# Where the convolution taps of a hybrid encoder block stand in VectorE's queue

## The chip, the cores and the metric

The kernel runs on one core of a Trainium2 chip. A core has five engines that run their own queues in order and wait for each other by semaphores: TensorE (PE in the profile, matmuls and transposes; PEld its weight loads), VectorE (DVE), ScalarE (ACT), GpSimd (POOL) and SyncE (SP, which only issues DMAs here). The metric is the device time of one execution in microseconds; lower is better. The number to be predicted is the median of the changed kernel's runs, on the same terms as the median of the kernel before.

## What is computed

One encoder layer on 1024 tokens of width 1024, in float32. Two head groups share one input projection: a convolution group (gated, 31 taps over positions, layer norm, swish) and a neighbourhood attention on a 16 x 64 grid of tokens. Their outputs are concatenated, projected, and a SwiGLU feed-forward follows.

```python
h = rms_norm(x, norm1_g[l])
z = h @ w_in[l]
a, gate, q, k, v = jnp.split(z, splits, axis=-1)
conv_out = conformer_conv(a, gate, dw_kernel[l], dw_bias[l], conv_ln_g[l], conv_ln_b[l])
q = rms_norm(q.reshape(B, S, N_HEADS, HEAD_DIM), q_norm_g[l])
k = rms_norm(k.reshape(B, S, N_HEADS, HEAD_DIM), k_norm_g[l])
attn_out = neighbourhood_attention(q, k, v.reshape(B, S, N_HEADS, HEAD_DIM), rpb[l])
x = x + jnp.concatenate([conv_out, attn_out], axis=-1) @ w_out[l]
h = rms_norm(x, norm2_g[l])
x = x + (jax.nn.silu(h @ w_gate[l]) * (h @ w_up[l])) @ w_down[l]

# in conformer_conv
u = a * jax.nn.sigmoid(gate)
y = conv over positions of u, 31 taps per channel, + dw_bias; layer_norm; silu
```

## The kernel before

Every float32 product is made of three matmuls on a high and a low half of each operand (`mac`, L112 to L114). `split` makes the halves: a ScalarE cast (L104) and a subtraction (L108), on GpSimd for the weights of this stage. Weights are split one chunk at a time by `take()`, in a fixed order.

The stage that matters here is the input projection, up to about 250 us of the span. TensorE makes, one after the other, groups of 24 matmuls (8 blocks of the inner dimension, 3 each):

- key tiles, `project(1, t, head_post)`, t = 0 to 7, 128 tokens each (the first four stand before and among the first gates);
- gate and value halves of the four channel blocks of the convolution, `glu_step(c, h, part, ...)`, c = 0 to 3;
- query tiles, `project(0, t, head_post)`, t = 0 to 7; after each even t a `take()` splits one of the four chunks w20 to w23 of the value weights;
- value tiles, `value(t)`, t = 0 to 7, which read those four chunks in turn, k = 0 to 7, two blocks for each chunk. The first two score matmul pairs (L610) stand ahead of `value(6)` and `value(7)`.

Nothing schedules the instructions but the order in which the Python code issues them. `step(post)` runs the work that belongs to the group before: one group lies between a tile's matmuls and its post-processing. For a key or query tile that is `head_post`: eight ScalarE squares with their sums and a root (`head_sq`, L371, L374), then on VectorE a reciprocal, a scaling and the product zn (`head_scale`, L379, L380, L382). zn is transposed on TensorE (`head_T`, zt, L389) at the end of the group after the next, and ScalarE copies it to qT or kT (L394, L396). For a gate it is a product with the row scales (L442), ScalarE's sigmoid (L443) and a second product (L444); the other half then gives `u` (L450).

The convolution's 31 taps of each of the four channel blocks are done on the side, in two places:

- `conv_taps` does 24 of them on VectorE, in one accumulator `cv` in PSUM: a first product with the bias (L313), 23 multiply-adds (L318), then the sum with the other part (L323). `pump(n)` issues the next n of these, wherever it is called. It stops early where the next block's `u` isn't there yet.
- `side_taps` does the other 7 (SIDE): a product on ScalarE (L343, the first of a block L340) and an add on GpSimd (L344; the first has none). `side()` issues the next one; `step` calls it once at its end.

What is left of the taps is issued by `pump(200)` after `value(5)`, ahead of the first score step (`score_exp`, L623), which takes scores from PSUM, adds the bias table and finds the largest. Score matmuls write into the four PSUM buffers `mm` that the tiles use too, in turn; the second score pair has to wait for a buffer that the first score step frees.

Behind this stage come the attention proper, the output projection and the feed-forward, none of which the change touches. In the changed kernel the same lines stand two or three lines lower (L610 is L613, L623 is L626).

Of the kernel before, what the change touches and what calls it, by code (L numbers as in the profile page):

```python
# [67 lines left out]
def build(ctx, tc, a):  # L68
# [10 lines left out]
    def G(name, dt=F32):  # L79
        return T("G", [P, 1024], 22, name, dt)  # L80
# [7 lines left out]
    def ST(name, dt=F32):  # L88
        return T("st", [P, 512], 5, name, dt)
# [4 lines left out]
    def mm(name):  # L94
        return ps.tile([P, 512], F32, tag="mm", bufs=4, name=name)
# [14 lines left out]
    def mac(acc, l, r, start, stop):  # L110
        (lh, ll), (rh, rl) = l, r
        pe.matmul(acc, lh, rh, start=start, stop=False, skip_group_check=True)  # L112
        pe.matmul(acc, lh, rl, start=False, stop=False, skip_group_check=True)  # L113
        pe.matmul(acc, ll, rh, start=False, stop=stop, skip_group_check=True)  # L114
# [4 lines left out]
    def weave():  # L119
        if woven:  # L120
            woven.pop(0)()
# [228 lines left out]
    def side():  # L350
        next(sides, None)
# [3 lines left out]
    def pump(n):  # L355
        for _ in range(n):
            if not next(conv, False):
                return
# [4 lines left out]
    def head_sq(n, t, z):  # L363
        sq, ss = ST(f"sq{n}{t}"), SM(f"s{n}{t}")
        r = r1[:, t:t + 1]
        if n == 1 and t < 4:
            act.activation(sq, z, AF.Square, scale=r)
            dve.tensor_reduce(ss, sq.rearrange("p (h d) -> p h d", d=HD), mybir.AxisListType.X, OP.add)
        else:
            for h in range(NH):  # L370
                act.activation(sq[:, h * HD:(h + 1) * HD], z[:, h * HD:(h + 1) * HD], AF.Square, scale=r,  # L371
                               accum_out=ss[:, h:h + 1])
        sd = SM(f"d{n}{t}")
        act.activation(sd, ss, AF.Sqrt, bias=eps, scale=1.0 / HD)  # L374
        return sd

    def head_scale(n, t, z, sd):
        r = SM(f"r{n}{t}")
        dve.reciprocal(r, sd)  # L379
        dve.tensor_scalar(r, r, r1[:, t:t + 1], None, op0=OP.mult)  # L380
        zn = ST(f"zn{n}{t}")
        dve.tensor_tensor(zn.rearrange("p (h d) -> p h d", d=HD), z.rearrange("p (h d) -> p h d", d=HD),  # L382
                          r[:, :, None].to_broadcast([P, NH, HD]), OP.mult)
        return zn

    def head_T(n, t, zn):
        pt = tp(f"zt{n}{t}")
        for c in range(4):
            pe.transpose(pt[:, c * P:(c + 1) * P], zn[:, c * P:(c + 1) * P], ident)  # L389
        if n == 0:  # L390
            q5 = qT.rearrange("p c (h b i j) -> p c h b i j", h=2, b=4, j=16)
            p5 = pt.rearrange("p (c i b j) -> p c i b j", c=4, i=2, j=16)
            for i in range(2):
                act.activation(q5[:, :, t // 4, :, 2 * (t % 4) + i, :], p5[:, :, i], AF.Copy, scale=qgs)  # L394
        else:
            act.activation(kT[:, :, t * P:(t + 1) * P], pt.rearrange("p (c s) -> p c s", s=P), AF.Copy, scale=kg)  # L396
# [11 lines left out]
    def step(post=None, n_taps=4):  # L408
        todo = pend[:]
        pend.clear()  # L410
        if post is not None:
            pend.append(post)
        behind()
        for f in todo:
            f(n_taps)
        if not todo:
            pump(n_taps)
        side()

    def head_post(n, t, z):  # L420
        def f(n_taps):
            sd = head_sq(n, t, z)
            pump(2)
            zn = head_scale(n, t, z, sd)
            pump(1)
            woven.extend([lambda: None] * 7)
            woven.append(lambda: head_T(n, t, zn))
        return f

    def glu_step(c, h, part, accs, extra=None):  # L430
        acc = accs[part] = mm(f"gl{c}{h}{part}")
        w = [q.rearrange("p (k m) -> p k m", m=P) for q in wag[1 - part, c][0]]
        for k in range(KB):
            mac(acc, [q[:, k, :] for q in w], [q[:, k, :] for q in hT[h]], k == 0, k == KB - 1)
            weave()
        if extra:
            extra(0)

        def gate(n_taps):
            sg = accs["sg"] = ST(f"sg{c}{h}")  # L440
            row = rb[0][:, h * 512:(h + 1) * 512]
            dve.tensor_tensor(sg, acc, row, OP.mult)  # L442
            act.activation(sg, sg, AF.Sigmoid)  # L443
            dve.tensor_tensor(sg, sg, row, OP.mult)  # L444
            pump(n_taps - 1)

        def val(n_taps):
            if h == 0:
                u.append([G(f"u{c}"), False])
            dve.tensor_tensor(u[c][0][:, h * 512:(h + 1) * 512], acc, accs["sg"], OP.mult)  # L450
            u[c][1] = h == 1
            pump(3)
        step((gate, val)[part])
# [749 lines left out]
    for s, p in enumerate(SEQ):  # L1203
        for k in range(QF - 2):
            n = s * QF + k
# [34 lines left out]
```

## Time and profile before

| | us |
|---|---|
| median of 3 runs | 1081.25 (1081.23 to 1082.03) |
| the profiled execution | 1082.53 |
| its span, first to last instruction | 1080.8 |
| TensorE busy in the span | 1056.1 |
| VectorE busy | 699.0 |
| ScalarE busy | 451.9 |
| GpSimd busy | 392.3 |

The span is what the profile's rows cover. In a row of a timeline stand the start and the duration in us, engine, source line, operation, the tiles written and read, shapes, the number of instructions merged into the row, and in square brackets how long the engine had idled before and what ended that. In a row of the waits stand the total in us, the number of waits and the longest. In a row of the view by windows stand, after the stretch and its length, the busy us and the number of instructions of TensorE, its weight loads, VectorE, ScalarE and GpSimd, then TensorE's granted clock as a share of full speed, the busy share of the DMA engines and their GB/s. TensorE's busy time is modelled from starts, so it overlaps from one matmul to the next: two starts say more than one duration.

### The profile page before, as it was taken

How to read it: one execution, taken by the hardware profiler on the slowest of the kernel's cores; microseconds unless marked ns; L12 is line 12 of the kernel's file. 1: busy time of each engine (PE TensorE's matmuls, PEld its weight loads, DVE VectorE, ACT ScalarE, POOL GpSimd, SP SyncE). 2: the span in 40 equal slices, each digit the busy share in tenths (PEclk: the TensorE clock that was granted, in tenths of full speed). 3: DMA queues.
4: the chain of work that ended last, by engine and by line, in shares of the span. 5: the costliest groups of instructions: out<-in, count | busy, mean ns of one | idle time of the engine just before them, and what ended most of it. 6: DMA issues, size and time to landing. Idle time of an engine off the chain costs nothing.

```text
span 1080.8 us, 14055 instructions
## 1 busy us (share of the span) xinstructions
PE 1056.1 (98%) x5068; PEld 850.7 (79%) x5068; DVE 699.0 (65%) x1055; ACT 451.9 (42%) x988; POOL 392.3 (36%) x303
## 2 busy tenths in 40 slices
PE   7999999989999999999999999999999999999997
PEld 5888888866667888788888888888888888888886
DVE  6768997895765346765646555464564667857883
ACT  6455347725775423533222332223322245433441
POOL 0126665513552301744454544544545300002310
PEclk9999999999999999999999999999999999999999
DMA  8416781234413522022321323322232498624641
GB/s 320 169 48 220 228 243 39 74 143 144 149 59 108 161 102 86 34 88 107 125 100 69 128 97 107 107 98 91 104 126 79 156 333 289 204 88 129 205 133 41
DMA packets 68245, 144.06 MB, mean 133 GB/s; under 512 B 12496, under 2 KB 21200, under 8 KB 67536
## 3 DMA queue, kind: packets, MB, share of 16 engines
q1 hardware_dynamic: 66336, 139.95, 38.3%
q10 hardware_dynamic: 1840, 3.22, 0.9%
q8 instruction: 40, 0.66, 0.2%
q14 instruction: 29, 0.24, 0.1%
HBM read 103.99 MB, written 44.76 MB: 138 GB/s over the span
## 4 chain that ended last, share of the span: by engine, by line
PE 90%; DVE 5%; ACT 3%; issue 1%; DMA 1%; POOL 0%; SPq 0%; ACTq 0%; DVEq 0%
PE B L112 6%; PE B L114 6%; PE B L113 6%; PE D L112 4%; PE D L114 4%; PE D L113 4%; PE A L112 4%; PE A L114 4%; PE A L113 4%; PE z L112 3%; PE z L113 3%; PE z L114 3%; DVE cv L318 3%; PE gl L112 3%; PE gl L114 3%; PE gl L113 3%
## 5 line engine op out<-in xcount | busy, mean ns | idle before, releaser
L318 DVE SCALAR_TENSOR_TENSOR cv<-u,par,cv 128x1009 f32<-128x1009 f32 (+14 forms) x92 | 117.5, 1277 | 2.5
L344 POOL TENSOR_TENSOR pa<-pa,pr 128x1022 f32<-128x1022 f32 (+5 forms) x24 | 57.5, 2395 | 53.8 <-ACT pr L343 53.4
L104 ACT CAST op<-sr 128x512 fp32r<-128x512 f32 x77 | 47.6, 618 | 52.3 <-PE B2d L114 23.2
L1027 DVE TENSOR_TENSOR g<-B,g 128x512 f32<-128x512 f32 x22 | 15.2, 690 | 80.3 <-PE B L114 80.3
L108 DVE TENSOR_TENSOR op<-sr,op 128x512 fp32r<-128x512 f32 x77 | 55.5, 721 | 16.4 <-ACT op L104 16.2
L1195 POOL TENSOR_TENSOR ou<-ou,resm 128x512 f32<-128x512 f32 x8 | 12.9, 1614 | 143.4 <-DMA resm<-xd 142.1
L1036 ACT ACTIVATE D<-D 128x512 f32<-128x512 f32 x22 | 12.8, 582 | 114.5 <-DVE D L1035 114.5
L1022 DVE TENSOR_TENSOR u<-B,g 128x512 f32<-128x512 f32 x22 | 15.2, 691 | 64.5 <-PE B L114 64.5
L104 ACT CAST op<-wd 128x512 fp32r<-128x512 f32 x66 | 40.8, 619 | 30.6 <-DVE wd L1114 18.1
L108 DVE TENSOR_TENSOR op<-wd,op 128x512 fp32r<-128x512 f32 x66 | 52.3, 793 | 2.0 <-ACT op L104 0.2
L876 DVE TENSOR_TENSOR ts<-gu,ts 128x512 f32<-128x512 f32 x44 | 53.1, 1206 | 0.8
L632 POOL TENSOR_SCALAR e<-e,rs 128x288 f32<-128x288 f32 (+1 forms) x64 | 34.1, 545 | 50.4 <-DVE rs L630 37.6
L1025 ACT ACTIVATE A<-A 128x512 f32<-128x512 f32 x20 | 11.6, 582 | 77.4 <-PE A L114 77.4
L625 ACT ACTIVATE e<-e,mx 128x288 f32<-128x288 f32 (+1 forms) x64 | 36.2, 568 | 14.1 <-DVE mx L623 14.1
L641 PEld LDWEIGHTS p<-ident,e 128*96 128x96 f32 (+1 forms) x192 | 20.0, 133 | 18.6 <-issue 10.3
L876 DVE TENSOR_TENSOR ts<-gu 128x512 f32<-128x512 f32 x22 | 33.6, 1528 | 0.0
L623 DVE CUSTOM_DVE_ANT_0 e<-s,tab 128x288 f32<-128x288 f32 (+1 forms) x64 | 29.8, 502 | 5.6 <-PE s L610 5.2
L610 PE MATMUL s<-kT,qT 64*128 64x288 f32 (+1 forms) x128 | 27.6, 496 | 3.8 <-DVE mx L623 3.8
L641 PE MATMUL p<-ident,e 128*96 128x128 f32 (+1 forms) x192 | 27.5, 280 | 3.8 <-DVE pT L646 2.5
L371 ACT ACTIVATE sq<-z,r 128x64 f32<-128x64 f32 x96 | 28.6, 333 | 2.8 <-PE z L114 2.8
L657 PE MATMUL o<-pT,vw 96*64 96x128 f32 (+1 forms) x384 | 28.0, 281 | 0.0
L343 ACT ACTIVATE pr<-u,par 128x1022 f32<-128x1022 f32 (+5 forms) x24 | 27.0, 1137 | 1.6 <-ACT vs L402 1.6
(1034 smaller groups left out, 3469.4 us busy)
## 6 DMA issues: line engine op xcount, KB each, us to landing
gu<-in_gu SPq DMA_DIRECT2D x44, 512.0 KB
sr<-sd SPq DMA_DIRECT2D x77, 256.0 KB
sd<-sd SPq DMA_DIRECT2D x22, 512.0 KB
wd<-in_wd SPq DMA_DIRECT2D x44, 256.0 KB
sd<-g SPq DMA_DIRECT2D x33, 256.0 KB
x<-in_x SPq DMA_DIRECT2D x16, 512.0 KB
xd<-x SPq DMA_DIRECT2D x8, 512.0 KB
resm<-xd SPq DMA_DIRECT2D x16, 256.0 KB
```

Source lines behind the costliest of these rows:

```text
L104: act.copy(hi, src)
L108: eng.tensor_tensor(*[w[..., sl] for w in (lo, src, hi.bitcast(F32))], OP.subtract)
L112: pe.matmul(acc, lh, rh, start=start, stop=False, skip_group_check=True)
L113: pe.matmul(acc, lh, rl, start=False, stop=False, skip_group_check=True)
L114: pe.matmul(acc, ll, rh, start=False, stop=stop, skip_group_check=True)
L318: dve.scalar_tensor_tensor(acc[:, o], uc[:, i], dwk[:, c, t:t + 1], acc[:, o], OP.mult, OP.add)
L344: pool.tensor_tensor(pa[:, o], pa[:, o], pr[:, o], OP.add)
L623: dve.tensor_tensor_reduce(out=e[:, hh], in0=ss[hh], in1=tab[rh, cb][2 * hp + hh], scale=-1.0, scalar=3.0e38, op0=OP.add, op1=OP.min, accu ...
L625: act.activation(e[:, hh], e[:, hh], AF.Exp, bias=mx, scale=-1.0, accum_out=rs[:, hh:hh + 1])
L632: pool.tensor_scalar(es[i][:, hh], es[i][:, hh], rs[:, hh:hh + 1], 1.0, op0=OP.mult, op1=OP.mult)
L641: pe.transpose(pt[:m, g * P:(g + 1) * P], es[i][:, hh, g * m:(g + 1) * m], ident)
L876: dve.tensor_tensor(o, l, r, OP.subtract)
```

## The change

Three places issue the same work in another order. A key or query tile pumps three taps in place of two before `head_scale` (six for key tile 5, five for query tile 1); after it, an odd tile pumps one as before and an even tile none. An odd query tile issues one more side tap. A gate pumps one of its taps between the issue of the sigmoid and the product that needs it. The number of taps and their arithmetic stay as they were.

```diff
     def head_post(n, t, z):
         def f(n_taps):
             sd = head_sq(n, t, z)
-            pump(2)
+            pump(3 + {(1, 5): 3, (0, 1): 2}.get((n, t), 0))
             zn = head_scale(n, t, z, sd)
-            pump(1)
+            pump(t % 2)
+            if n == 0 and t % 2:
+                side()
             woven.extend([lambda: None] * 7)
             woven.append(lambda: head_T(n, t, zn))
         return f
...
             dve.tensor_tensor(sg, acc, row, OP.mult)
             act.activation(sg, sg, AF.Sigmoid)
+            pump(1)
             dve.tensor_tensor(sg, sg, row, OP.mult)
-            pump(n_taps - 1)
+            pump(n_taps - 2)
```

## The prediction

> **What bounds the kernel now.** I read the page first, then the list of waits (TensorE's over the span, VectorE's from 56 to 262 us), then the timeline of each engine around the one wait that the change can reach. A difference of 0.2% (2.16 us) is about what a measurement of this kernel can tell from no change.
>
> ```profile
> PE 1056.1 (98%) x5068; PEld 850.7 (79%) x5068; DVE 699.0 (65%) x1055; ACT 451.9 (42%) x988; POOL 392.3 (36%) x303
> ...
> PE s L610 <- DVE mx L623: 3.8, 1, 3.8
> PE p L641 <- DVE pT L646: 2.5, 5, 0.6
> PE A L112 <- ACT g L1019: 1.9, 1, 1.9
> ...
> DVE r L379 <- ACT d L374: 15.8, 10, 5.3
> DVE sg L444 <- ACT sg L443: 8.4, 8, 2.1
> ```
>
> TensorE (PE) is the bound: it is busy for 1056.1 of 1080.8 us, and its largest wait in mid-kernel is a single one of 3.8 us, for a VectorE (DVE) score step. Only time of TensorE is worth anything here. VectorE's own waits for head squares (15.8 us) and sigmoids (8.4 us) cost nothing by themselves; they matter because VectorE is late at that one place. TensorE's timeline there:
>
> ```profile
> 229.24 0.76 PE L610 MATMUL s<-kT,qT 64*128 64x288 f32 x4
> ...
> 235.71 0.75 PE L610 MATMUL s<-kT,qT 64*128 64x288 f32 x2
> 240.26 0.90 PE L610 MATMUL s<-kT,qT 64*128 64x288 f32 x2 [3.80 <-DVE mx L623]
> ...
> 242.53 0.63 PE L112 MATMUL z<-w20h,hT 128*128 128x512 f32 x1
> 242.96 0.63 PE L113 MATMUL z<-w20l,hT 128*128 128x512 f32 x1
> ...
> 248.26 0.76 PE L610 MATMUL s<-kT,qT 64*128 64x288 f32 x4
> ```
>
> One pair of score matmuls and one value tile take 235.71 - 229.24 = 6.47 us when nothing is in the way. The next pair and tile take 248.26 - 235.71 = 12.55 us. So the wait costs 12.55 - 6.47 = **6.08 us**, not 3.80: another 2.28 us go afterwards, where matmuls start 0.43 us apart (242.53, 242.96). The view by windows shows why; the column behind the five engines is the granted clock:
>
> ```profile
> 236.00:240.00 4.00, 0.46 (x2) 0.01 (x1) 3.86 (x4) 0.00 (x0) 0.00 (x0) 1.00 0.02 8
> 240.80:244.00 3.20, 3.20 (x8) 2.33 (x8) 1.07 (x6) 2.36 (x9) 1.00 (x3) 0.50 0.22 82
> 244.20:248.00 3.80, 3.80 (x18) 3.00 (x16) 0.00 (x0) 0.00 (x0) 0.77 (x2) 1.00 0.00 0
> ```
>
> VectorE is late because it still works off the last convolution channel:
>
> ```profile
> 204.48 0.20 DVE L379 RECIPROCAL r<-d 128x8 f32<-128x8 f32 x1 [0.98 <-ACT d L374]
> ...
> 205.06 0.69 DVE L382 TENSOR_TENSOR zn<-z,r 128x512 f32<-128x512 f32 x1
> 205.66 1.21 DVE L323 TENSOR_TENSOR u<-cv,pa 128x1024 f32<-128x1024 f32 x1
> ...
> 208.30 30.21 DVE L318 SCALAR_TENSOR_TENSOR cv<-u,par,cv 128x1009 f32<-128x1009 f32 x23
> 238.61 1.22 DVE L323 TENSOR_TENSOR u<-cv,pa 128x1024 f32<-128x1024 f32 x1
> 239.75 0.45 DVE L623 CUSTOM_DVE_ANT_0 e<-s,tab 128x288 f32<-128x288 f32 x1
> ```
>
> 23 taps (30.21 us) stand between the last query tile (zn at 205.06) and the first score step (239.75), while inside the tiles before, VectorE idles 0.98 us each time for ScalarE's squares.
>
> **Taps into the waits.** The change adds no VectorE work, it reorders it. By program order 26 instructions follow the last zn before the first score step (a sum, a first product, 23 taps, a sum); afterwards there are 19: 18 taps and a sum. A query tile gets 3 taps (even t) or 4 (odd t) in place of 3, and t = 1 gets 2 more; key tile 5 gets 7 in place of 3. One tap is 30.21 / 23 = 1.313 us, so what follows the last zn takes 18 x 1.313 + 1.14 (238.61 to 239.75) = 24.8 us: begun at 205.66 it ends at 230.4 instead of 239.75. The score row that waits for it can run from 235.71 + 0.35 = 236.1 on. VectorE is then over 5 us early; the 3.80 us are gone, TensorE does not idle there and has no reason to lose its clock: **-6.08 us**. What is late next at that place is TensorE itself.
>
> **One more side tap in odd query tiles.** It puts a second product (L343) on ScalarE and a second add (L344) on GpSimd between the squares of an odd tile and the next weight split (L104, L108). The moved steps issue no DMA. At the last such place, behind the squares of t = 5, the split is that of w23, and TensorE needs its low half soon:
>
> ```profile
> 192.06 0.30 ACT L374 ACTIVATE d<-s,eps 128x8 f32<-128x8 f32 x1
> 192.27 1.13 ACT L340 ACTIVATE pa<-u,par 128x1023 f32<-128x1023 f32 x1
> 193.31 1.03 ACT L104 CAST w23h<-w23r 128x1024 fp32r<-128x1024 f32 x1
> 194.86 0.84 ACT L394 ACTIVATE qT<-zt,qgs 128x256 f32<-128x256 f32 x2 [0.52 <-PE zt L389]
> ...
> 198.31 1.13 ACT L343 ACTIVATE pr<-u,par 128x1022 f32<-128x1022 f32 x1
> ...
> 194.47 2.39 POOL L108 TENSOR_TENSOR w23l<-w23r,w23h 128x1024 fp32r<-128x1024 f32 x1 [4.56 <-issue]
> 199.52 2.40 POOL L344 TENSOR_TENSOR pa<-pa,pr 128x1022 f32<-128x1022 f32 x1 [2.66 <-ACT pr L343]
> ...
> 199.10 0.39 PE L113 MATMUL z<-w23l,hT 128*128 128x512 f32 x1
> ```
>
> Before, this slot holds a channel's first product (L340), which has no GpSimd add, and GpSimd takes w23l at 194.47. In the new program order GpSimd has two adds ahead of w23l. The first can start 199.52 - 198.31 = 1.21 us after its product: 192.27 + 1.21 = 193.48. Two adds of 2.40 end at 198.28, and w23l at 198.28 + 2.39 = 200.67. How long GpSimd's end takes to reach TensorE:
>
> ```profile
> 281.21 0.98 POOL L632 TENSOR_SCALAR e<-e,rs 128x288 f32<-128x288 f32 x2
> ...
> 282.33 0.83 PE L641 MATMUL p<-ident,e 128*96 128x128 f32 x6 [0.36 <-POOL e L632]
> ```
>
> 282.33 - 282.19 = 0.14 us. TensorE can go on at 200.81, where it wanted to at 199.10: **+1.70 us**, a new wait inside the first value tile. TensorE's queue behind it is the rest of that tile, which waits with it, and everything later moves by it, also the last zn (230.4 becomes 232.1, still early). Bounds: 0, if the adds start earlier than I read; not below, since TensorE does not wait there before; and 2.7, if ScalarE's products slip by another 1.0.
>
> **Transposes of the query tiles.** Behind an odd tile's squares ScalarE now has two products and a cast, 0.21 + 1.04 + 1.04 + 1.03 = 3.32 us from 192.06: the next qT starts at 195.38, 0.52 after 194.86, and the squares, the root and r behind it are 0.52 late. In VectorE's queue four taps then stand ahead of an even tile's r: 4 x 1.313 + 1.18 (204.48 to 205.66) = 6.43 us, against the 6.04 of a tile (the two zt rows below); that alone would be 0.39, so ScalarE's 0.52 rules. The room:
>
> ```profile
> 186.35 0.20 DVE L379 RECIPROCAL r<-d 128x8 f32<-128x8 f32 x1 [0.94 <-ACT d L374]
> ...
> 186.93 0.69 DVE L382 TENSOR_TENSOR zn<-z,r 128x512 f32<-128x512 f32 x1
> ...
> 182.15 0.60 PE L389 MATMUL zt<-ident,zn 128*128 128x128 f32 x4
> 188.19 0.60 PE L389 MATMUL zt<-ident,zn 128*128 128x128 f32 x4
> ```
>
> zn ends at 187.62 and, with the same 0.14, is at TensorE by 187.76; the transpose runs at 188.19. Room 0.43, so t = 2 and t = 4 cost 0.52 - 0.43 = 0.09 each (t = 6 lies behind the new wait): **+0.2 us**, between 0 and 0.6. The taps in the key tiles and between a gate's product and its sigmoid's return I take at nothing: they fill VectorE's own waits, and by the list TensorE waits for no key tile and no gate. Were that cover gone, a key tile with four taps ahead would pay the same few tenths, which the 0.6 holds.
>
> **Sum.** -6.08 + 1.70 + 0.2 = -4.18. The profiled execution took 1082.53 us (a span of 1080.8 and 1.73 around it), 1.28 above the median of the runs. On the median of 1081.25 the forecast is **1077.1 us**; in an execution like the profiled one it is a span of 1076.6.
>
> **Does the new wait cost clock as well?** The row to go by is TensorE's other wait:
>
> ```profile
> 435.20 0.74 PE L112 MATMUL A<-h,t0m 128*128 128x512 f32 x1 [1.95 <-ACT g L1019]
> ...
> 438.72 0.40 PE L114 MATMUL A<-h,t0m 128*128 128x512 f32 x1
> 436.00:438.50 2.50, 2.50 (x7) 1.92 (x7) 2.46 (x3) 0.15 (x1) 2.50 (x3) 0.50 0.00 0
> ```
>
> After only 1.95 us of idling the clock was 0.50 until 438.72; 3.52 us at half clock lose 1.76. The waits of up to 0.6 us in the attention show nothing of it. 1.70 lies nearer to 1.95 but is shorter, so the loss is a rival. The Trainium skill (TensorE: Matmul & The Clock Gate, "What's actually happening") halves the clock only after an idle window of about 3.4 us. By that rule the new wait costs no clock and the forecast stands as it is; the wait of 3.80 us agrees, the one of 1.95 us contradicts the rule, and the measurement decides.
>
> **The rivals.**
> - The new wait halves the clock: 1.76 as at 435, up to the 2.28 at 240: 1078.9. For it the row at 435.20, against it the shorter wait. 0.16.
> - Better: GpSimd is not late with w23l, 1077.1 - 1.70 = 1075.4; or the wait at 435, which comes at another moment, keeps its clock, 1077.1 - 1.76 = 1075.3. Nothing in the rows above speaks for the first; the second can't be excluded. Together 0.14.
> - The change doesn't do what it says: the first score step gets no earlier, as something else holds it, its bias table above all, whose buffers are handed on in another order. Then 6.08 stay and 1.9 come on top: 1083.2. Against it: no row shows VectorE waiting for a table before. 0.04.
> - Slower: VectorE becomes the bound of the query tiles. Two tiles hold 7 taps and 2 x 1.18, 11.55 of 12.08 us. From a tap of 1.39 us on, TensorE waits at the transposes; at 1.65 it waits 1.8 per two tiles, 7.3 in all, and the time is 1084.4. Against it: 1.313 is what a tap took, and the change puts no more beside it than one product and one add in two tiles. 0.04.
>
> **How the numbers follow.** The forecast has 0.62. Faster by over 0.2% means below 1079.1: the forecast, the better cases and the clock rival but for its dear end, 0.88. Within 0.2%, up to 1083.4: that end and the table, 0.08. Slower: 0.04. The range leaves out the last two rivals; it goes from 1074.9 (a better case without the 0.2, and 0.2 for the scatter of runs) to 1079.3 (the clock rival with the 0.6 of the transposes).
>
> **What would show it.** Right: no TensorE wait at the score matmuls near 236 and clock 1.00 behind them; a TensorE wait of about 1.7 us for w23l near 199; 18 taps in a row of 23.6 us that end near 231. Wrong: the score wait again, over 0.6 us of TensorE waits at zt, or clock 0.50 behind 200.

## The result, and the profile after

The change made the kernel slower: 1084.78 us in the median of 22 runs (1082.64 to 1086.59) against 1082.75 of the kernel before (22 runs beside them, 1081.23 to 1084.49), a ratio of 1.0021 with a 95% interval of 1.0014 to 1.0028. The forecast was 1077.1 us, 4.2 less than the median of the three runs that it started from; measured are 2.0 more than the kernel before timed beside it. The profiled execution of the kernel after took 1086.28 us, 1.5 above its median, with a span of 1084.6.

The list of waits of the kernel after, TensorE over the span and VectorE from 56 to 262 us as before (engine, tile and line, what it waited for; us in total, times, longest):

```profile
PE zt L389 <- DVE zn L382: 6.0, 3, 2.4
...
PE z L113 <- POOL w23l L108: 1.5, 1, 1.5
...
DVE r L379 <- ACT d L374: 7.1, 6, 3.4
```

The score wait of 3.8 us is off TensorE's list, and VectorE's waits for squares fell from 15.8 to 7.1 us: the taps did move into them. VectorE's timeline ahead of the first score step:

```profile
215.53 23.65 DVE L318 SCALAR_TENSOR_TENSOR cv<-u,par,cv 128x1014 f32<-128x1014 f32 x18
239.28 1.22 DVE L323 TENSOR_TENSOR u<-cv,pa 128x1024 f32<-128x1024 f32 x1
240.43 0.45 DVE L626 CUSTOM_DVE_ANT_0 e<-s,tab 128x288 f32<-128x288 f32 x1
```

18 taps instead of 23. What is new is 6.0 us of waiting for zn, at three transposes. Timelines of VectorE, of GpSimd and of TensorE in the kernel after, around the first two:

```profile
68.64 0.20 DVE L379 RECIPROCAL r<-d 128x8 f32<-128x8 f32 x1
68.88 1.62 DVE L380 TENSOR_SCALAR r<-r,r 128x8 f32<-128x8 f32 x1
...
71.21 7.85 DVE L318 SCALAR_TENSOR_TENSOR cv<-u,par,cv 128x1014 f32<-128x1014 f32 x6
78.97 0.20 DVE L379 RECIPROCAL r<-d 128x8 f32<-128x8 f32 x1
79.20 2.17 DVE L380 TENSOR_SCALAR r<-r,r 128x8 f32<-128x8 f32 x1
81.48 0.69 DVE L382 TENSOR_TENSOR zn<-z,r 128x512 f32<-128x512 f32 x1
...
87.47 2.41 DVE L380 TENSOR_SCALAR r<-r,r 128x8 f32<-128x8 f32 x1
...
68.08 2.39 POOL L344 TENSOR_TENSOR pa<-pa,pr 128x1022 f32<-128x1022 f32 x1 [1.73 <-ACT pr L343]
78.99 2.36 POOL L344 TENSOR_TENSOR pa<-pa,pr 128x1021 f32<-128x1021 f32 x1 [8.52 <-DMA t<-in_rpb]
87.49 2.36 POOL L344 TENSOR_TENSOR pa<-pa,pr 128x1020 f32<-128x1020 f32 x1 [3.82 <-ACT pr L343]
...
82.23 0.66 PE L389 MATMUL zt<-ident,zn 128*128 128x128 f32 x4 [2.25 <-DVE zn L382]
90.82 0.63 PE L389 MATMUL zt<-ident,zn 128*128 128x128 f32 x4 [2.43 <-DVE zn L382]
...
92.33 0.63 PE L112 MATMUL gl<-hT,ag01h 128*128 128x512 f32 x1
92.75 0.63 PE L113 MATMUL gl<-hT,ag01h 128*128 128x512 f32 x1
```

L380 multiplies 128x8 numbers, r by r1. The prediction never named it: it lies between r and zn and takes 0.23 us. Here it takes 1.62, 2.17 and 2.41 us. Its end is each time 0.02 to 0.03 us behind that of the GpSimd add L344 beside it (68.88 + 1.62 = 70.50 and 68.08 + 2.39 = 70.47). The first delay costs TensorE nothing by itself, but it pushes six taps and the next r (78.97) into the next add (78.99). The reciprocal L379 runs at 68.64 in the middle of the same add and still takes 0.20 us. TensorE waits 2.25 and 2.43 us, and behind the second wait its matmuls start 0.42 to 0.43 us apart. The view by windows shows the granted clock there (column behind the five engines), 1.00 behind the first wait and 0.59 behind the second:

```profile
82.30:85.70 3.40, 3.40 (x17) 2.87 (x18) 3.33 (x3) 2.78 (x16) 1.38 (x1) 1.00 1.02 399
91.00:94.20 3.20, 3.20 (x12) 2.59 (x11) 3.13 (x3) 2.71 (x16) 0.00 (x0) 0.59 0.51 147
```

The third wait, and the one for w23l, in the query and the value tiles (GpSimd, VectorE, TensorE):

```profile
180.76 2.39 POOL L108 TENSOR_TENSOR w21l<-w21r,w21h 128x1024 fp32r<-128x1024 f32 x1
206.44 2.37 POOL L108 TENSOR_TENSOR w23l<-w23r,w23h 128x1024 fp32r<-128x1024 f32 x1
...
181.47 1.70 DVE L380 TENSOR_SCALAR r<-r,r 128x8 f32<-128x8 f32 x1
...
184.11 0.63 PE L389 MATMUL zt<-ident,zn 128*128 128x128 f32 x4 [1.30 <-DVE zn L382]
208.87 0.50 PE L113 MATMUL z<-w23l,hT 128*128 128x512 f32 x1 [1.55 <-POOL w23l L108]
```

The additional side tap made the weight splits late, as forecast for w23; it made w21l late too, and L380 stood behind that one. Behind w23l stood one more L380 (207.14, 1.70 us), and no wait of TensorE for zn came of it.

The trace of before had it all, once. VectorE and GpSimd in the kernel before:

```profile
158.97 1.75 DVE L380 TENSOR_SCALAR r<-r,r 128x8 f32<-128x8 f32 x1
...
158.31 2.38 POOL L344 TENSOR_TENSOR pa<-pa,pr 128x1021 f32<-128x1021 f32 x1 [4.21 <-ACT pr L343]
...
78.11 0.23 DVE L380 TENSOR_SCALAR r<-r,r 128x8 f32<-128x8 f32 x1
...
79.02 2.40 POOL L344 TENSOR_TENSOR pa<-pa,pr 128x1021 f32<-128x1021 f32 x1 [8.35 <-ACT pr L343]
```

At 158.97 L380 ran into an add and took 1.75 us, and nobody waited for it. Elsewhere, as at 78.11, VectorE stood waiting for ScalarE's d and ran L380 as soon as d came, 0.91 us ahead of the add, which has to wait for a ScalarE product that is issued behind d. The wait that the change fills with taps was what kept L380 clear of GpSimd.

### The profile page after: what moved, and what is told of

Its sections match the earlier page's. It is cut to its first block, busy times and chain, and to the rows that moved or that the text cites. A ratio compares the mean times of both kernels' runs of the same rounds, so it can differ in the third digit from the quotient of the medians.

```text
span 1084.6 us, 14053 instructions
## 1 busy us (share of the span) xinstructions
PE 1057.3 (97%) x5068; PEld 850.3 (78%) x5068; DVE 706.7 (65%) x1055; ACT 451.8 (42%) x988; POOL 391.5 (36%) x303
## 4 chain that ended last, share of the span: by engine, by line
PE 86%; DVE 7%; ACT 4%; issue 1%; POOL 1%; DMA 0%; SPq 0%; DVEq 0%; ACTq 0%; POOLq 0%
PE B L112 6%; PE B L114 6%; PE B L113 6%; PE D L112 4%; PE D L114 4%; PE D L113 4%; PE A L112 4%; PE A L114 4%; PE A L113 4%; PE z L112 3%; PE z L113 3%; PE z L114 3%; PE p L644 2%; PE gl L114 2%; PE gl L112 2%; PE gl L113 2%
## 5 line engine op out<-in xcount | busy, mean ns | idle before, releaser
L344 POOL TENSOR_TENSOR pa<-pa,pr 128x1022 f32<-128x1022 f32 (+5 forms) x24 | 57.5, 2397 | 62.0 <-ACT pr L343 53.0
L108 DVE TENSOR_TENSOR op<-sr,op 128x512 fp32r<-128x512 f32 x77 | 58.2, 756 | 15.7 <-ACT op L104 15.6
```

The costliest lines, as they stand in the source:

```text
L108: eng.tensor_tensor(*[w[..., sl] for w in (lo, src, hi.bitcast(F32))], OP.subtract)
L344: pool.tensor_tensor(pa[:, o], pa[:, o], pr[:, o], OP.add)
```

## The experiments

Theory A: L380 stands still while a GpSimd instruction runs, and taps ahead of r push it into one. Theory B: VectorE's queue in the key tiles is simply too long. Medians are compared with the kernel before, timed beside each (1082.4 to 1082.8 us).

**L380 taken out, in the kernel after** (1077.31 us, ratio 0.9953, 0.9941 to 0.9965).

```diff
-        dve.tensor_scalar(r, r, r1[:, t:t + 1], None, op0=OP.mult)
         zn = ST(f"zn{n}{t}")
-        dve.tensor_tensor(zn.rearrange("p (h d) -> p h d", d=HD), z.rearrange("p (h d) -> p h d", d=HD),
-                          r[:, :, None].to_broadcast([P, NH, HD]), OP.mult)
+        dve.scalar_tensor_tensor(zn.rearrange("p (h d) -> p h d", d=HD), z.rearrange("p (h d) -> p h d", d=HD),
+                                 r1[:, t:t + 1], r[:, :, None].to_broadcast([P, NH, HD]), OP.mult, OP.mult)
```

> The kernel after, with one instruction of VectorE taken out of each head tile: the small multiply r = r * r1 (L380) goes, and its factor is taken along in the multiply that makes zn, now (z * r1) * r in one scalar_tensor_tensor. Order of the taps and slots as in the kernel after.
> Theory A (the small multiply on VectorE stands still while a GpSimd instruction runs; the taps ahead of it push it into one): the three waits of TensorE for zn (2.25, 2.43 and 1.30 us, 6.0 together) and the half clock behind the second (some 1.7 us) go: about 7.7 us less than after, 1077.1 us, 0.995 of before; every instruction that makes zn takes 0.6 to 0.8 us, beside GpSimd or not. The wait of 1.5 us for w23l stays.
> Theory B (with three to six taps ahead of r the queue of VectorE is simply too long in key tiles 1 and 2, whatever the small multiply takes): the waits for zn stay at over 4 us, the time within 1 us of after (1084.8).

All three waits for zn are gone and the time is that of theory A; of the new waits only the one for w23l is left. The new multiply reads z from PSUM and r from SBUF. VectorE and GpSimd at the place where L380 took 1.62 us, and TensorE's wait for w23l from the list:

```profile
68.83 0.75 DVE L381 SCALAR_TENSOR_TENSOR zn<-z,r,r 128x512 f32<-128x512 f32 x1
...
68.02 2.39 POOL L344 TENSOR_TENSOR pa<-pa,pr 128x1022 f32<-128x1022 f32 x1 [1.78 <-ACT pr L343]
...
PE z L113 <- POOL w23l L108: 1.6, 1, 1.6
```

It runs through in 0.75 us while the add is running.

**The same in the kernel before** (1081.64 us, 0.9991, 0.9982 to 0.9999).

> The same fusion in the kernel before (L380 out, its factor taken along in the multiply that makes zn); nothing else. A control: what the fusion is worth where the small multiply meets GpSimd only once (158.97, 1.75 us, with no wait of TensorE behind it).
> Theory A: within 0.5 us of before, 1082.7: the wait of 3.80 us at the score matmul and the half clock behind it stay. Theory B: the same. If it is faster by over 2 us, the fusion has a worth of its own, and the gain of the other run is not that of the blocked multiply.

About 1 us, more than the 0.5 expected; the score wait stays (3.6 us). So of the 7.5 us that the fusion brings in the kernel after (1084.78 - 1077.31) about 1 is its own; by the interval it is between 0.1 and 1.9.

**Without the additional side slot, in the kernel after** (1082.63 us, 0.9999, 0.9991 to 1.0008).

```diff
-            if n == 0 and t % 2:
-                side()
```

> The kernel after without the additional slot for a side tap in the odd query tiles; taps of VectorE and gate as in after.
> The prediction's term (the side tap delays the weights w23l on GpSimd): the wait of 1.5 us for w23l at the first value tile goes. Theory A besides: the wait for zn at 184 (1.30 us), where the small multiply stood behind the split of w21l, which came late in the same way, goes too; those at 82 and 91 and the half clock stay: 1.5 to 2.8 us less than after, 1082.0 to 1083.3 us. Theory B: only the 1.5 us, and the wait at 184 stays. Against both: the side taps end later and TensorE waits for s again, up to the 3.8 us of before.

2.15 us less than after; the two waits that go are 1.55 and 1.30, and the difference lies within the intervals. The wait for w23l is gone and so is the one at 184: w21l is split 2.8 us sooner than in the kernel after, and L380 finds GpSimd idle (GpSimd, VectorE):

```profile
177.97 2.42 POOL L108 TENSOR_TENSOR w21l<-w21r,w21h 128x1024 fp32r<-128x1024 f32 x1
...
181.03 0.23 DVE L380 TENSOR_SCALAR r<-r,r 128x8 f32<-128x8 f32 x1
```

The two waits in the key tiles stay (4.6 us), and the score wait does not come back.

**Same number of taps in the key tiles, two of them ahead of r** (1084.59 us, 1.0015, 1.0005 to 1.0024).

```diff
-            pump(3 + {(1, 5): 3, (0, 1): 2}.get((n, t), 0))
+            late = {(1, 5): 3, (0, 1): 2}.get((n, t), 0)
+            pump(2 if n else 3 + late)
...
-            pump(t % 2)
+            pump(1 + t % 2 + late if n else t % 2)
```

> The kernel after, where in the eight key tiles the same number of taps is issued (3, 4, ... as in after), but only two of them ahead of r as in before, and the others behind zn. Query tiles and gate as in after.
> Theory A: r waits for ScalarE's d again in the key tiles, the small multiply runs ahead of GpSimd's instruction in 0.23 us; the waits for zn at 82 and 91 (4.7 us) and the half clock (1.7 us) go: 1078.4 us; the waits at 184 and for w23l stay. Theory B (the number of taps in the queue, not their place ahead of r, makes zn late): the waits for zn stay within 1 us of 6.0, the time within 1 us of after.

A miss. Every L380 of the key tiles takes 0.23 us and the wait at 82 is gone, as theory A has it, but there is a longer wait at 90 (VectorE, TensorE, and the window behind the wait):

```profile
79.61 9.19 DVE L318 SCALAR_TENSOR_TENSOR cv<-u,par,cv 128x1016 f32<-128x1016 f32 x7
...
90.11 0.63 PE L389 MATMUL zt<-ident,zn 128*128 128x128 f32 x4 [3.50 <-DVE zn L382]
90.10:93.50 3.40, 3.39 (x17) 2.90 (x18) 3.33 (x3) 2.73 (x16) 0.00 (x0) 1.00 0.61 163
```

The five taps behind zn of tile 5 and the two ahead of the next r make seven in a row, 9.19 us: theory B's mechanism exists, and the design of this run brought it in. It doesn't tell the theories apart.

**GpSimd's adds left out for the first channel block** (1079.34 us, 0.9974, 0.9964 to 0.9984). VectorE's queue is that of the kernel after.

```diff
-                    pool.tensor_tensor(pa[:, o], pa[:, o], pr[:, o], OP.add)
+                    if c > 0:
+                        pool.tensor_tensor(pa[:, o], pa[:, o], pr[:, o], OP.add)
```

> The kernel after with the GpSimd additions of the side taps (L344) left out for the first of the four channel groups, so that those side taps are not added up; VectorE's and ScalarE's instructions, their order and number are as in after, with the small multiply L380 and up to six taps ahead of it.
> Theory A (L380 stands still while a GpSimd instruction runs): with nothing on GpSimd at 68.9, 79.2 and 87.5 the three long L380 take 0.23 us each; the waits for zn at 82 and 91 (4.7 us) and the half clock behind the second (1.7 us) go: 1078.4 us. The wait at 184 and the one for w23l, which hang on the later groups and on the splits of weights, stay.
> Theory B (the number of taps in VectorE's queue makes zn late, whatever GpSimd does): both waits stay, the time within 1 us of after, 1084.8.

This does. The same taps stand ahead of the same r, GpSimd has nothing to do beside them, and the two waits are gone. The multiply (line 381 here) in tiles where it took 2.17 and 2.41 us, and a new collision (VectorE, GpSimd, TensorE):

```profile
77.54 0.23 DVE L381 TENSOR_SCALAR r<-r,r 128x8 f32<-128x8 f32 x1
83.86 0.23 DVE L381 TENSOR_SCALAR r<-r,r 128x8 f32<-128x8 f32 x1
...
334.56 2.31 DVE L750 SCALAR_TENSOR_TENSOR bb<-bm,br 128x1 f32<-128x1 f32 x1
...
334.48 2.38 POOL L108 TENSOR_TENSOR wo<-wo02r,wo 128x1024 fp32r<-128x1024 f32 x1 [3.15 <-ACT wo L104]
...
337.82 0.66 PE L723 MATMUL y<-ident,u 128*128 128x128 f32 x4 [1.46 <-ACT xh L751]
```

The 0.9 us above the expectation probably come from that: the multiply of 128x1 numbers in the convolution's layer norm (the expectations further down call it batch norm), in a stage that the change doesn't touch, meets a weight split and takes 2.31 us instead of 0.16, and TensorE waits 1.46 us there, where the kernel after has no wait over 0.4 us.

**L380 as tensor_tensor, in the kernel after** (1082.20 us, 0.9995, 0.9986 to 1.0004).

```diff
-        dve.tensor_scalar(r, r, r1[:, t:t + 1], None, op0=OP.mult)
+        dve.tensor_tensor(r, r, r1[:, t:t + 1].to_broadcast([P, NH]), OP.mult)
```

> The kernel after with the small multiply in another form: tensor_tensor of r and r1 (both read from SBUF, r1 by broadcast) in place of tensor_scalar with r1 as its scalar. All else as in after.
> Theory A1 (it is the form tensor_scalar that GpSimd's instruction shuts out): the multiply takes 0.2 to 0.3 us beside GpSimd too, the waits for zn and the half clock go, 1077.3 us as in the fused kernel.
> Theory A2 (whatever reads two operands from SBUF and writes there waits; the product L447, which does, took 1.27 us beside GpSimd in before, where it takes 0.69 alone): the multiply still takes 1.5 to 2.5 us in the same places, the time stays within 1 us of after, 1084.8. I hold A2 the likelier, 6 to 4.

```profile
78.11 2.19 DVE L380 TENSOR_TENSOR r<-r,r 128x8 f32<-128x8 f32 x1
86.40 0.17 DVE L380 TENSOR_TENSOR r<-r,r 128x8 f32<-128x8 f32 x1
...
77.93 2.35 POOL L344 TENSOR_TENSOR pa<-pa,pr 128x1021 f32<-128x1021 f32 x1 [8.54 <-ACT pr L343]
86.58 2.40 POOL L344 TENSOR_TENSOR pa<-pa,pr 128x1020 f32<-128x1020 f32 x1 [3.98 <-ACT pr L343]
...
81.50:84.50 3.00, 3.00 (x10) 2.42 (x9) 2.93 (x3) 2.49 (x14) 1.10 (x1) 0.50 1.03 400
```

Two operands from SBUF are shut out as well: the wait at 81 (2.24 us) and the one at 180 stay, and the half clock now stands behind the one at 81 (the window above). The wait at 90 went by a hair: the multiply began 0.18 us ahead of the add and got through; in the kernel after it began 0.02 us ahead (87.47 and 87.49) and did not. The 2.6 us less than after are about that one wait (2.43), which is why the time lies between the two expectations.

**The gate alone, in the kernel before** (1081.85 us, 1.0001, 0.9992 to 1.0009): the gate lines of the change and nothing else.

> The kernel before with one part of the change alone: in the gates one tap stands between the sigmoid and the product, and one fewer behind it. Head tiles as in before.
> The prediction took this part at nothing: VectorE's waits for ScalarE's sigmoids (8.4 us in before) shrink, but the number of taps left over ahead of the score matmul is the same, and so are the wait of 3.80 us there and the half clock: 1082.8 us within 0.5. Rival: a tap ahead of the product, which reads two operands from SBUF, pushes it into a GpSimd instruction as it does the small multiply of the head tiles: products of over 1 us, and up to 2 us slower.

Nothing, as forecast, by the ratio, though the median lies 0.8 us below that of the kernel before beside it (1082.62). Three of the products take 1.3 to 2.9 us beside GpSimd, where two took 1.1 and 1.3 in the kernel before, but TensorE's list of waits is that of before.

**Fused, and without the additional side slot** (1075.83 us, 0.9937, 0.9924 to 0.9949): the first and the third edit together.

> Both at once: the kernel after with the small multiply fused into the one that makes zn, and without the additional slot for a side tap in the odd query tiles.
> The two terms add: 1077.3 of the fused kernel less the wait of 1.6 us for w23l: 1075.7 us, 0.9935 of before, with no wait of TensorE over 0.75 us between 30 and 430 us. Rival: without the slot the side taps end late and the score matmul waits for VectorE again, by up to 3.8 us and a half clock: 1079 us or more.

The terms add; TensorE's longest wait from 30 to 427 us is 0.6; the next, 1.95 at 428, is the one that stands at 435 in the kernel before.

**Key tiles with two taps ahead of r, and without the three additional taps of tile 5** (1079.87 us, 0.9977, 0.9967 to 0.9987).

```diff
-            pump(3 + {(1, 5): 3, (0, 1): 2}.get((n, t), 0))
+            pump(2 if n else 3 + {(0, 1): 2}.get((n, t), 0))
...
-            pump(t % 2)
+            pump(1 + t % 2 if n else t % 2)
```

> The kernel after, with two taps ahead of r in every key tile as in before, one or two behind zn (1 + t % 2), and without the three additional taps of key tile 5, which in the run with seven taps between two r made zn late by themselves. Query tiles and gate as in after.
> Theory A (the place of the taps ahead of r pushes L380 into GpSimd's instruction): all L380 of the key tiles take 0.23 us, the waits for zn at 82 and 91 (4.7 us) and the half clock (1.7 us) go: 1078.4 us; the waits at 184 and for w23l stay. The three taps are left over ahead of the score matmul: 21 in place of 18, 3.9 us more of VectorE, and since VectorE waits 4.11 us for TensorE behind its first two score rows in after, no wait there, or one under 0.5 us.
> Theory B (the key tiles have no room for more than three taps each): a wait for zn of over 1 us stays somewhere between 80 and 100 us, the time over 1080 us.
> Rival on the score matmul: the three taps bring its wait back, up to 3.9 us, 1082 us.

No wait for zn between 80 and 100; 1.5 us above the expectation, and the 128x1 multiply met a weight split again, with a wait of 1.5 us at 338. The count was wrong in a telling way: 18 taps are left over (23.64 us from 208.91), not 21. The three taps of key tile 5 never reach the score step. They end the first channel block sooner, and then `pump` stops, since the second block's u comes only with its gate and value groups.

**The key tiles' taps alone, in the kernel before** (1087.16 us, 1.0047, 1.0034 to 1.0060).

```diff
-            pump(2)
+            pump((6 if t == 5 else 3) if n else 2)
...
-            pump(1)
+            pump(t % 2 if n else 1)
```

> The kernel before with one part of the change alone: in the key tiles the taps of the kernel after (three, in tile 5 six, ahead of r; one behind zn in odd tiles). Query tiles and gates as in before.
> Theory A: this part only loses. Its taps bring the first channel group to its end sooner, but the second can't begin before its gate, and by program order the same 23 taps are left over ahead of the score matmul: the wait of 3.8 us there and the half clock stay. L380 meets GpSimd in the key tiles as in after: waits for zn of 4.7 us in all near 82 and 91, and a half clock of some 1.6 us: 1082.6 + 6.3 = 1088.9 us, and not under 1086.
> Rival (the key tiles' taps are part of what took away the score wait): the score wait gets under 2 us, 1085 us or less.

A loss of 4.5 us. TensorE's list and VectorE's timeline ahead of the score step:

```profile
PE zt L389 <- DVE zn L382: 4.7, 2, 2.4
PE s L610 <- DVE mx L623: 2.5, 1, 2.5
...
208.28 1.23 DVE L323 TENSOR_TENSOR u<-cv,pa 128x1024 f32<-128x1024 f32 x1
...
211.04 0.69 DVE L382 TENSOR_TENSOR zn<-z,r 128x512 f32<-128x512 f32 x1
...
213.02 30.21 DVE L318 SCALAR_TENSOR_TENSOR cv<-u,par,cv 128x1009 f32<-128x1009 f32 x23
```

The 23 taps are still there. TensorE and the last zn both come 5.98 us later than before (zn at 211.04, there at 205.06), so lateness alone would leave the score wait as it was. It is 1.26 us shorter since one instruction did get ahead: the sum of the third channel block (L323) stands ahead of the last zn, where the kernel before has it behind (205.66). So 25 instructions follow in place of 26.

**The change without its two losing parts, L380 untouched** (1075.56 us, 0.9931, 0.9917 to 0.9944): the key tiles as two experiments above, and no additional side slot.

> The kernel after, without what the runs so far showed to lose: key tiles with two taps ahead of r and one or two behind zn, and no additional slot for a side tap; the small multiply L380 stays as it is. Query tiles' taps and gates as in after.
> Theory A: every L380 takes 0.23 us, no wait for zn over 0.75 us, none for w23l, none at the score matmul: 1076 to 1077.5 us, within 1.5 us of the fused kernel without the slot (1075.8); up to 1.5 us more if the small batch norm multiply near 335 meets GpSimd as it did in the run with two taps.
> Rival: query tiles with three to five taps ahead of r push L380 into GpSimd there as well: a wait for zn over 1 us between 155 and 215 us, 1078 us or more.

```profile
PE z L112 <- ACT wk0h L104: 7.7, 1, 7.7
PE p L642 <- DVE pT L647: 2.5, 5, 0.6
PE A L112 <- ACT g L1020: 2.0, 1, 2.0
```

The first wait is the one for the first weights, which all of these kernels have (6.4 to 7.8 us). Every L380 takes 0.23 us, and no wait for zn, w23l or the score step is left. 7.1 us less than before (1082.65 beside it), by the order of taps alone; it beats both kernels, and can't be told from the fused version.

## Why the prediction was wrong

**Taps into the waits, -6.08: right.** The score wait and its half clock went, with 18 taps of 23.65 us in a row as forecast. The fused kernels with and without the change's taps, both without the additional slot, differ by 1075.83 - 1081.64 = -5.8. What brings it are the taps in the query tiles. By program order they alone would leave 20 of the 26 instructions behind the last zn. The key tiles' taps alone leave 25 and the gate lines alone 26, as their runs show, and without the three taps of key tile 5 there are 19 as in the kernel after. The query tiles' taps by themselves were not run.

**One more side tap, +1.70: the wait itself was right** (1.55 in the list of after, 1.80 from start to start; 1077.31 - 1075.83 = 1.5 with L380 fused). Missing was its second effect, w21l late and L380 behind it, 1.30 us at 184; the slot cost 2.15 us in the medians.

**Transposes, +0.2 with at most 0.6: this step failed.** It costs 2.25 + 2.43 + 1.30 = 6.0 us of waits, of which the 1.30 needs the side slot as well. The half clock behind 90.82 adds, for the nine starts from 91.21 to 94.89, 3.68 us in place of 9 x 0.23 = 2.07, so 1.6: together 7.6. The fusion took away 7.5, about 1 of it its own, so the sizes agree only to about 1 us. The key tiles' taps alone, in the kernel before, cost 4.5 us in the median. The +0.2 for the query tiles' own transposes was no mistake: apart from the one at 184 they lost at most 0.03 us each. The sentence that failed is the one that took the taps in the key tiles "at nothing: they fill VectorE's own waits". It looked for who waits for VectorE and how many taps fit. That was no mistake in the count: with GpSimd's adds left out even the six taps ahead of r make nobody wait. It took the instructions between r and zn at the length that they had beside an idle GpSimd, from the rows at 204.48 to 205.66, and did not ask what else runs at the moment to which they are moved. The row at 158.97 showed the price.

The Trainium skill (SBUF — State Buffer, "Who interferes with whom") states the mechanism. VectorE and GpSimd share a pair of SBUF ports, and whoever issues first has it for the whole instruction while the other waits. On VectorE this concerns tensor_scalar in its two-port modes, and any instruction with two SBUF inputs beside a GpSimd instruction that reads SBUF; one with at most one SBUF input, outside those modes, does not wait. The traces agree: tensor_scalar 2.17 us, tensor_tensor 2.19, the reciprocal with one input 0.20, the multiply that takes z from PSUM 0.75. That L380 ran in such a mode, and that it is these ports and nothing else between the two engines, no run here can show; that GpSimd's instruction is what L380 waits for is shown by leaving the adds out.

**The sum.** From the transpose at 73.8 us, which both kernels reach at the same time, to 251 us the kernel after falls back by 3.8 us. The steps with the waits as listed give -6.08 + 1.55 + 5.98 + 1.6 = 3.1. The other 0.7 is in how a wait is counted: from the modelled end of the matmul before it, 0.40 us after its start, where the next would have started after 0.23. Counted from start to start against the same stretches of the kernel before, the four waits cost 2.40, 2.55, 1.46 and 1.80 us; with 1.6 for the half clock and -6.06 at the score matmuls that makes 3.8. In medians it is 2.0, since the profiled execution of the kernel after lay 1.5 above its median and that of before 0.2 below. **The clock rival** of the new wait did not come: behind 1.55 us the clock was 1.00. **VectorE as the bound** did not come either: a tap took 23.65 / 18 = 1.31 us. The prediction's own sign was there ("over 0.6 us of TensorE waits at zt"), for a reason that no rival named.

## What to carry to other kernels

Before filling an engine's idle time, ask what that idle time keeps apart: an instruction that waits for its input at a fixed distance ahead of another engine's instruction may owe its short duration to that. Look in the trace for the longest, not only the mean, duration of each small VectorE instruction that you move, and at what GpSimd does in that moment. And count by program order whether work that is moved forward arrives at the wait that it is to shorten: of the key tiles' taps no more than one instruction did.

## What the runs showed of the hardware

A VectorE multiply of 128x8 or 128x1 numbers with its operands in SBUF waits out a GpSimd add or subtraction of 2.4 us that runs beside it: 0.23 became up to 2.41 us, 0.16 became 2.31. In one case each, a start 0.18 us ahead of the add was enough to escape and one 0.02 us ahead was not.

Whether a wait halves TensorE's clock does not follow from its length alone. Waits of 2.43 us (clock 0.59 behind it), 2.24 (at 81 in the run with tensor_tensor, 0.50 behind it) and 1.95 (at 435 in the kernel before) did; 2.25 us at 82.23 and the 3.50 us at 90.11 in the run with seven taps in a row did not, and in the fused kernel without the slot the wait of 1.95 us at 428.12 did not either:

```profile
428.50:432.00 3.50, 3.50 (x19) 2.89 (x18) 3.47 (x3) 0.58 (x2) 3.50 (x3) 1.00 0.00 0
```

The Trainium skill (TensorE: Matmul & The Clock Gate, "What's actually happening") has a window of 3413 ns that runs freely and lets the moment at which the clock changes depend on where in the window the first matmul falls. If the same holds for an idle stretch, which is my inference, the mixed outcomes fit; the Trainium skill's threshold of one idle window does not fit the halving behind 1.95, 2.24 and 2.43 us. The scatter goes with the clock: of the kernel with seven taps in a row, one execution took 1081.41 us at a mean granted clock of 0.999 and another 1086.51 at 0.994.
